# A 4096 x 4096 matrix product on one core: panels of half the width, chunked loads, and a transposed A kept in memory

## The chip, the core and the metric

The kernel runs on one core of one Trainium2 chip. Times are device microseconds from the first to the last work of a launch. TensorE (PE in the profile) multiplies and transposes, VectorE (DVE) copies, ScalarE (ACT) scales, GpSimd (POOL) issues the casting loads, and SyncE (SP) issues the other transfers. The accumulators that TensorE writes are PSUM tiles, everything else on the core is SBUF; `a`, `b` and `out` lie in the chip's memory.

## The reference

```python
def setup_inputs():
    m, k, n = 4096, 4096, 4096
    return {
        "a": np.random.randn(m, k).astype(np.float32),
        "b": np.random.randn(k, n).astype(np.float32),
        "scale": np.float32(0.1),
    }

def reference(a, b, scale):
    return np.matmul(a, b) * scale
```

## The kernel before, in words

B is cut into two panels of 2048 columns (`NB`, L27). For each panel one load from GpSimd's queue brings all 4096 rows into one SBUF tile and casts them to bf16 (L51). That tile has a single buffer, so the second panel's load waits until the first panel's last matmul is done. Inside a panel the loop runs over 32 blocks of 128 rows of A (L53). For each block:

- a load from GpSimd's queue brings 128 x 4096 of A, cast to bf16 (L56), into one of two buffers;
- TensorE transposes it in 32 pieces of 128 x 128 into PSUM tiles `pt` (L61), and VectorE copies each piece to the tile `at_sb` (L62); there are four `pt` buffers and two `at_sb` buffers;
- 4 x 32 matmuls of 128 x 512 (L67) add up into the one accumulator `po` of 128 x 2048, four column pieces one after the other;
- ScalarE multiplies `po` by the scale into `o_sb` (L76), and SyncE stores 1 MB of output (L77).

Each block of A is thus loaded and transposed twice, once for each panel. A scheduler orders each engine's instructions from this program and adds the waits; it puts the first transposes of a block ahead of and among the block's first matmuls. The single accumulator makes a block's first matmul wait for the scaling of the block before.

Of the kernel before, what the change touches and what calls it, by code (L numbers as in the profile page):

```python
# [1 line left out]

# [5 lines left out]


@with_exitstack
def kernel(
    ctx: ExitStack,
    tc: tile.TileContext,
    a: bass.AP,
    b: bass.AP,
    scale: float,
    out: bass.AP,
):
    nc = tc.nc  # L20
    P = 128
    M, K = a.shape
    K2, N = b.shape
    assert K == K2

    KO = K // P
    NB = 2048  # L27
    NPANELS = N // NB
    NSUB = NB // 512
    MB = M // P  # L30

    fp32 = mybir.dt.float32
    bf16 = mybir.dt.bfloat16

    b_r = b.rearrange("(ko ki) n -> ki ko n", ki=P)

    const = ctx.enter_context(tc.tile_pool(name="const", bufs=1))
    bpool = ctx.enter_context(tc.tile_pool(name="bpool", bufs=1))
    apool = ctx.enter_context(tc.tile_pool(name="apool", bufs=2))
    atpool = ctx.enter_context(tc.tile_pool(name="atpool", bufs=2))  # L40
    opool = ctx.enter_context(tc.tile_pool(name="opool", bufs=3))
    psum_o = ctx.enter_context(tc.tile_pool(name="psum_o", bufs=1, space=bass.MemoryType.PSUM))
    psum_t = ctx.enter_context(tc.tile_pool(name="psum_t", bufs=4, space=bass.MemoryType.PSUM))

    ident = const.tile([P, P], bf16)
    make_identity(nc, ident)

    for pi in range(NPANELS):
        n0 = pi * NB
        b_sb = bpool.tile([P, KO, NB], bf16, tag="bpanel")  # L50
        nc.gpsimd.dma_start(out=b_sb, in_=b_r[:, :, n0:n0 + NB])  # L51

        for mi in range(MB):  # L53
            m0 = mi * P
            a_sb = apool.tile([P, K], bf16, tag="arow")
            nc.gpsimd.dma_start(out=a_sb, in_=a[m0:m0 + P, :])  # L56

            at_sb = atpool.tile([P, KO, P], bf16, tag="at")
            for ko in range(KO):
                pt = psum_t.tile([P, P], bf16, tag="pt")  # L60
                nc.tensor.transpose(pt, a_sb[:, ko * P:(ko + 1) * P], ident)  # L61
                nc.vector.tensor_copy(at_sb[:, ko, :], pt)  # L62

            po = psum_o.tile([P, NB], fp32, tag="po", bufs=1)
            for ns in range(NSUB):
                for ko in range(KO):
                    nc.tensor.matmul(  # L67
                        po[:, ns * 512:(ns + 1) * 512],
                        at_sb[:, ko, :],
                        b_sb[:, ko, ns * 512:(ns + 1) * 512],  # L70
                        start=(ko == 0),
                        stop=(ko == KO - 1),
                    )

            o_sb = opool.tile([P, NB], fp32, tag="osb")
            nc.scalar.mul(o_sb, po, float(scale))  # L76
            nc.sync.dma_start(out=out[m0:m0 + P, n0:n0 + NB], in_=o_sb)  # L77


# [1 line left out]
_INS = ['a', 'b', 'scale']  # L81
_OUTS = [((4096, 4096), 'float32')]
#: Inputs that are plain numbers.
_NUMBERS = {'scale': 0.10000000149011612}


# [26 lines left out]
```

## Time and profile before

| | |
|---|---|
| median of 4 runs | 2159.67 us (2159.45 to 2160.71) |
| profiled execution | 2159.5 us |
| its span, first to last instruction | 2157.7 us |
| TensorE busy | 1934.5 us |
| VectorE busy | 324.9 us |
| ScalarE busy | 121.4 us |
| read from memory, written | 201.33 MB, 67.11 MB |
| mean granted TensorE clock | 0.981 |

Busy time of TensorE counts from a matmul's start to its modelled end, and matmuls overlap each other in the array; the time that a matmul costs is therefore the distance from one start to the next. The recorded mean of 379 ns for a 128 x 512 matmul is not that distance. Weight loads (PEld) are recorded completely and run beside the matmuls; some matmul records are missing, so counts are taken from the weight loads. The bytes of a casting load are counted as written, that is, as bf16.

### The profile page before, as it was taken

The numbers are of one execution on the slowest core, as the hardware profiler recorded it, in microseconds if no ns is written. First come the engines' busy times: TensorE is split into PE (matmuls) and PEld (weight loads), VectorE is DVE, ScalarE is ACT, GpSimd is POOL, SyncE is SP. The second block draws the span as 40 slices with busy tenths as digits, with TensorE's granted clock in tenths as the row PEclk, the third lists the DMA queues.
The fourth block names the chain that finished last, engine by engine and source line by source line (L and its number), as shares of the span: only waits on it lengthen the run. The fifth ranks groups of instructions, "written<-read, shape, count | busy, mean of one in ns | idle before, by whom it ended". The sixth has DMA issues, their size and how long they took to land.

```text
span 2157.7 us, 22825 instructions
## 1 busy us (share of the span) xinstructions
PE 1934.5 (90%) x10048; PEld 942.1 (44%) x10240; DVE 324.9 (15%) x2048; ACT 121.4 (6%) x65; POOL 38.2 (2%) x72
## 2 busy tenths in 40 slices
PE   0399999999999999999914999999999999999998
PEld 0144444444444444444411444444444444444444
DVE  0011111111111111111010011111111101110110
ACT  0000000000000000000000000000000000000000
POOL 0000000000000000000000000000000000000000
PEclk9999999999999999999966999999999999999999
DMA  9821332233223322332297222332233223322320
GB/s 198 172 70 48 79 78 68 50 78 79 65 53 79 79 63 55 79 79 61 57 208 162 59 65 53 79 79 63 55 78 79 61 57 78 79 61 57 79 59 40
DMA packets 26756, 169.26 MB, mean 78 GB/s; under 512 B 2080, under 2 KB 2080, under 8 KB 10272
## 3 DMA queue, kind: packets, MB, share of 16 engines
q0 software_dynamic: 17440, 100.67, 24.5%
q1 hardware_dynamic: 9216, 67.11, 7.6%
q8 instruction: 80, 1.31, 0.2%
q14 instruction: 20, 0.16, 0.0%
HBM read 201.33 MB, written 67.11 MB: 124 GB/s over the span
## 4 chain that ended last, share of the span: by engine, by line
PE 86%; another core or an unknown queue 8%; ACT 5%; issue 1%; DVE 0%; ACTq 0%
PE po L67 82%; ACT o_sb L76 5%; PE pt L61 4%; DVE at_sb L62 0%; ACTq L76 0%
## 5 line engine op out<-in xcount | busy, mean ns | idle before, releaser
L67 PE MATMUL po<-b_sb,at_sb 128*128 128x512 bf16 x8000 | 1826.3, 379 | 115.4 <-DMA b_sb<-in_b_dram 77.7
L67 PEld LDWEIGHTS <-at_sb 128*128 128x128 bf16 x8192 | 799.4, 98 | 969.3 <-DMA b_sb<-in_b_dram 77.9
L62 DVE COPY at_sb<-pt 128x128 bf16<-128x128 bf16 x2048 | 324.9, 219 | 1801.2 <-PE pt L61 1795.3
L61 PE MATMUL pt<-ident,a_sb 128*128 128x128 bf16 x2048 | 284.2, 219 | 101.0 <-DMA a_sb<-in_a_dram 88.6
L61 PEld LDWEIGHTS <-a_sb 128*128 128x128 bf16 x2048 | 191.4, 98 | 239.1 <-DMA a_sb<-in_a_dram 88.6
L76 ACT ACTIVATE o_sb<-po 128x2048 f32<-128x2048 f32 x64 | 120.1, 1877 | 2030.8 <-PE pt L61 1825.3
L56 POOL DMA_DIRECT2D a_sb<-in_a_dram x64 | 34.0, 532 | 2000.8 <-PE pt L61 1969.1
L51 POOL DMA_DIRECT2D b_sb<-in_b_dram x2 | 3.5, 1762 | 25.1 <-PE pt L61 24.7
L76 ACT ACT_TABLE_LOAD x1 | 1.3, 1283 | 0.7 <-PEq L94 0.7
masks.py:199 POOL TENSOR_SCALAR_AFFINE_SELECT ident<-ident 128x128 bf16<-128x128 bf16 x1 | 0.3, 307 | 0.1
masks.py:197 POOL MEMSET ident<- 128x128 bf16 x1 | 0.2, 205 | 0.3 <-POOLq L94 0.3
L94 POOL MEMSET const-float32-0.0<- 128x1 f32 x1 | 0.1, 100 | 0.2 <-issue 0.2
L94 POOL MEMSET const-bfloat16-1.0<- 128x1 bf16 x1 | 0.1, 103 | 0.0
L94 POOL MEMSET const-uint8-127<- 128x1 uint8 x1 | 0.1, 102 | 0.0
L94 POOL MEMSET const-float32-1.0<- 128x1 f32 x1 | 0.1, 100 | 0.0
## 6 DMA issues: line engine op xcount, KB each, us to landing
a_sb<-in_a_dram POOLq DMA_DIRECT2D x64, 1024.0 KB, 7.6
out_dram<-o_sb SPq DMA_DIRECT2D x64, 1024.0 KB, 3.9
b_sb<-in_b_dram POOLq DMA_DIRECT2D x2, 16384.0 KB, 84.1
```

The source lines that it names most:

```text
L51: nc.gpsimd.dma_start(out=b_sb, in_=b_r[:, :, n0:n0 + NB])
L56: nc.gpsimd.dma_start(out=a_sb, in_=a[m0:m0 + P, :])
L61: nc.tensor.transpose(pt, a_sb[:, ko * P:(ko + 1) * P], ident)
L62: nc.vector.tensor_copy(at_sb[:, ko, :], pt)
L67: nc.tensor.matmul(po[:, ns * 512:(ns + 1) * 512], at_sb[:, ko, :], b_sb[:, ko, ns * 512:(ns + 1) * 512], start=(ko == 0), stop=(ko == KO ...
L76: nc.scalar.mul(o_sb, po, float(scale))
L94: nc = _bacc.Bacc("TRN2", target_bir_lowering=False, num_devices=1)
```

## The change

- Panels are 1024 columns wide, so there are four. A panel of B is no longer one tile but 32 chunks of 128 x 1024, each with its own load, in a pool of 64 chunks, which holds two panels.
- In the first panel the first three blocks of A are loaded and transposed, then their 3 x 2 matmuls follow each chunk of B as it lands (`WIDE`). The load of the fourth block stands between chunks 21 and 22, its transposes behind chunk 26.
- Four transposes write one PSUM tile of 128 x 4 x 128, and one copy of 128 x 512 empties it; there are two such tiles.
- Each transposed block of A is written to a tile in memory (`at_dram`) by SyncE in the first panel; in the other panels it is read back from there, and neither loaded nor transposed again. There are four buffers for it.
- In the first panel the transposes of block t + 2 are placed behind the matmuls of chunk 4 of block t. The chunks of the second panel are spread over the blocks of the first.
- There are three accumulators of 128 x 1024. A block's two column pieces alternate for each chunk.

The order of the row-block work on TensorE. In the names, `a_6` is the seventh block of A, `pt_6_8` the PSUM tile of its pieces from 8 on, `po_0_4` the accumulator of panel 0, block 4; the number behind is the program's own. Before, in the second block:

```order
L67 MATMUL po_413<-b_sb_81,at_sb_316 128x512
L61 LDWEIGHTS a_sb_314
L61 MATMUL pt_386<-ident_76,a_sb_314 128x128 [waits DVE_49]
L61 LDWEIGHTS a_sb_314
L61 MATMUL pt_389<-ident_76,a_sb_314 128x128 [waits DVE_49]
L67 LDWEIGHTS at_sb_316
```

With the change, in block 4 of panel 0:

```order
L113 MATMUL po_0_4_732<-b_0_5_250,at_0_4_573 128x512
L69 LDWEIGHTS a_6_743
L69 MATMUL pt_6_8_758<-ident_79,a_6_743 128x128 [waits DVE_49]
...
L113 LDWEIGHTS at_0_4_573
L113 MATMUL po_0_4_732<-b_0_6_252,at_0_4_573 128x512
L69 LDWEIGHTS a_6_743
L69 MATMUL pt_6_12_764<-ident_79,a_6_743 128x128 [waits DVE_49]
```

One or two transposes of the same block stood between matmuls, each waiting for a copy; now four transposes of the block two further stand between single matmuls, and the first of each four waits for a copy.

The order of the loads on GpSimd's queue at the start of the program (`b_0_21` is chunk 21 of panel 0). Before:

```order
L51 DMA b_sb_81<-in_b_dram 128x32x2048
masks.py:199 ISA
masks.py:199 AFFINE_SELECT ident_76<-ident_76 128x128
L56 DMA a_sb_83<-in_a_dram 128x4096
L56 DMA a_sb_314<-in_a_dram 128x4096
```

With the change, behind the loads of A blocks 0 to 2 and chunks 0 to 20:

```order
L52 DMA b_0_21_282<-in_b_dram 128x1024
L58 DMA a_3_284<-in_a_dram 128x4096
L52 DMA b_0_22_286<-in_b_dram 128x1024
...
L52 DMA b_0_31_304<-in_b_dram 128x1024
L58 DMA a_4_571<-in_a_dram 128x4096
L58 DMA a_5_655<-in_a_dram 128x4096
L58 DMA a_6_743<-in_a_dram 128x4096
L52 DMA b_1_0_849<-in_b_dram 128x1024
```

A's first block stood behind the whole panel of B; now three blocks of A stand ahead of it, a fourth inside it and the next three behind it.

The order on SyncE's queue. Before it held the 64 output stores alone. With the change, in the second panel (`at_1_4` is the reload for its block 4, `o_1_0` its block 0's output):

```order
L76 DMA at_1_4_4200<-at_dram_78 128x4096 [waits DMAHW4_49,PE_49]
L109 DMA out_0_dram<-o_1_0_4125 128x1024 [waits Activation_49]
L76 DMA at_1_5_4272<-at_dram_78 128x4096 [waits DMAHW6_49,PE_49]
L109 DMA out_0_dram<-o_1_1_4197 128x1024 [waits DMAHW7_49,Activation_49]
L76 DMA at_1_6_4344<-at_dram_78 128x4096 [waits DMAHW0_49,PE_49]
```

Each reload now stands ahead of the store of the block whose buffer it takes over, and waits for TensorE to be done with that block.

```diff
--- before.py
+++ after.py
@@ -24,7 +24,7 @@
     assert K == K2
 
     KO = K // P
-    NB = 2048
+    NB = 1024
     NPANELS = N // NB
     NSUB = NB // 512
     MB = M // P
@@ -32,49 +32,131 @@
     fp32 = mybir.dt.float32
     bf16 = mybir.dt.bfloat16
 
-    b_r = b.rearrange("(ko ki) n -> ki ko n", ki=P)
+    const = ctx.enter_context(tc.tile_pool(name="const", bufs=1))
+    dram = ctx.enter_context(tc.tile_pool(name="dram", bufs=1, space=bass.MemoryType.DRAM))
+    bpool = ctx.enter_context(tc.tile_pool(name="bpool", bufs=2 * KO))
+    apool = ctx.enter_context(tc.tile_pool(name="apool", bufs=3))
+    atpool = ctx.enter_context(tc.tile_pool(name="atpool", bufs=4))
+    opool = ctx.enter_context(tc.tile_pool(name="opool", bufs=3))
+    psum_o = ctx.enter_context(tc.tile_pool(name="psum_o", bufs=3, space=bass.MemoryType.PSUM))
+    psum_t = ctx.enter_context(tc.tile_pool(name="psum_t", bufs=2, space=bass.MemoryType.PSUM))
 
-    const = ctx.enter_context(tc.tile_pool(name="const", bufs=1))
-    bpool = ctx.enter_context(tc.tile_pool(name="bpool", bufs=1))
-    apool = ctx.enter_context(tc.tile_pool(name="apool", bufs=2))
-    atpool = ctx.enter_context(tc.tile_pool(name="atpool", bufs=2))
-    opool = ctx.enter_context(tc.tile_pool(name="opool", bufs=3))
-    psum_o = ctx.enter_context(tc.tile_pool(name="psum_o", bufs=1, space=bass.MemoryType.PSUM))
-    psum_t = ctx.enter_context(tc.tile_pool(name="psum_t", bufs=4, space=bass.MemoryType.PSUM))
+    at_dram = dram.tile([MB, P, KO, P], bf16)
 
     ident = const.tile([P, P], bf16)
     make_identity(nc, ident)
 
-    for pi in range(NPANELS):
+    def load_b_chunk(pi, ko):
         n0 = pi * NB
-        b_sb = bpool.tile([P, KO, NB], bf16, tag="bpanel")
-        nc.gpsimd.dma_start(out=b_sb, in_=b_r[:, :, n0:n0 + NB])
+        bt = bpool.tile([P, NB], bf16, tag="bc", name=f"b_{pi}_{ko}")
+        nc.gpsimd.dma_start(out=bt, in_=b[ko * P:(ko + 1) * P, n0:n0 + NB])
+        return bt
 
-        for mi in range(MB):
-            m0 = mi * P
-            a_sb = apool.tile([P, K], bf16, tag="arow")
-            nc.gpsimd.dma_start(out=a_sb, in_=a[m0:m0 + P, :])
+    def load_a(mi):
+        m0 = mi * P
+        a_tiles[mi] = apool.tile([P, K], bf16, tag="arow", name=f"a_{mi}")
+        a_ins[mi] = nc.gpsimd.dma_start(out=a_tiles[mi], in_=a[m0:m0 + P, :]).ins
 
-            at_sb = atpool.tile([P, KO, P], bf16, tag="at")
-            for ko in range(KO):
-                pt = psum_t.tile([P, P], bf16, tag="pt")
-                nc.tensor.transpose(pt, a_sb[:, ko * P:(ko + 1) * P], ident)
-                nc.vector.tensor_copy(at_sb[:, ko, :], pt)
+    def make_at_via_pe(mi):
+        if mi not in a_tiles:
+            load_a(mi)
+        a_sb = a_tiles.pop(mi)
+        at_sb = atpool.tile([P, KO, P], bf16, tag="at", name=f"at_0_{mi}")
+        for kg in range(0, KO, 4):
+            pt = psum_t.tile([P, 4, P], bf16, tag="pt", name=f"pt_{mi}_{kg}")
+            for j in range(4):
+                ko = kg + j
+                nc.tensor.transpose(pt[:, j, :], a_sb[:, ko * P:(ko + 1) * P], ident)
+            nc.vector.tensor_copy(at_sb[:, kg:kg + 4, :], pt)
+        nc.sync.dma_start(out=at_dram[mi], in_=at_sb)
+        return at_sb
 
-            po = psum_o.tile([P, NB], fp32, tag="po", bufs=1)
-            for ns in range(NSUB):
-                for ko in range(KO):
-                    nc.tensor.matmul(
-                        po[:, ns * 512:(ns + 1) * 512],
-                        at_sb[:, ko, :],
-                        b_sb[:, ko, ns * 512:(ns + 1) * 512],
-                        start=(ko == 0),
-                        stop=(ko == KO - 1),
-                    )
+    def load_at(pi, mi):
+        at_sb = atpool.tile([P, KO, P], bf16, tag="at", name=f"at_{pi}_{mi}")
+        nc.sync.dma_start(out=at_sb, in_=at_dram[mi])
+        return at_sb
 
-            o_sb = opool.tile([P, NB], fp32, tag="osb")
-            nc.scalar.mul(o_sb, po, float(scale))
-            nc.sync.dma_start(out=out[m0:m0 + P, n0:n0 + NB], in_=o_sb)
+    def produce_at(pi, mi):
+        if pi == 0:
+            return make_at_via_pe(mi)
+        return load_at(pi, mi)
+
+    iters = [(pi, mi) for pi in range(NPANELS) for mi in range(MB)]
+    T = len(iters)
+    AHEAD = 2
+
+    a_ins = {}
+    a_tiles = {}
+    b_tiles = {}
+    at_tiles = {}
+
+    WIDE = 3
+    for s in range(WIDE):
+        at_tiles[s] = produce_at(*iters[s])
+    latest = WIDE - 1
+    for ko in range(KO):
+        if ko == 22:
+            latest += 1
+            load_a(latest)
+        with tc.issue_after(a_ins[latest]):
+            b_tiles[(0, ko)] = load_b_chunk(0, ko)
+
+    def finish(pi, mi, po):
+        n0 = pi * NB
+        m0 = mi * P
+        o_sb = opool.tile([P, NB], fp32, tag="osb", name=f"o_{pi}_{mi}")
+        nc.scalar.mul(o_sb, po, float(scale))
+        nc.sync.dma_start(out=out[m0:m0 + P, n0:n0 + NB], in_=o_sb)
+
+    def mm(po, at, pi, ko):
+        for ns in range(NSUB):
+            i = nc.tensor.matmul(
+                po[:, ns * 512:(ns + 1) * 512],
+                at[:, ko, :],
+                b_tiles[(pi, ko)][:, ns * 512:(ns + 1) * 512],
+                start=(ko == 0),
+                stop=(ko == KO - 1),
+            )
+        return i.ins
+
+    # the first WIDE row blocks follow the chunks of B as they land
+    pos = [psum_o.tile([P, NB], fp32, tag="po", name=f"po_0_{w}") for w in range(WIDE)]
+    for ko in range(KO):
+        for w in range(WIDE):
+            ins = mm(pos[w], at_tiles[w], 0, ko)
+        if ko == 26:
+            with tc.issue_after(ins):
+                at_tiles[WIDE] = produce_at(*iters[WIDE])
+    for w in range(WIDE):
+        finish(0, w, pos[w])
+        at_tiles.pop(w)
+
+    nb = 0
+    for t in range(WIDE, T):
+        pi, mi = iters[t]
+        ahead = [WIDE + 1, WIDE + 2] if t == WIDE else [t + 2] if t + 2 < T else []
+        if pi > 0:
+            for s in ahead:
+                at_tiles[s] = produce_at(*iters[s])
+            ahead = []
+            if pi + 1 < NPANELS:
+                b_tiles[(pi + 1, mi)] = load_b_chunk(pi + 1, mi)
+
+        at_cur = at_tiles.pop(t)
+        po = psum_o.tile([P, NB], fp32, tag="po", name=f"po_{pi}_{mi}")
+        for ko in range(KO):
+            ins = mm(po, at_cur, pi, ko)
+            if ko in (4, 20) and ahead:
+                with tc.issue_after(ins):
+                    s = ahead.pop(0)
+                    at_tiles[s] = produce_at(*iters[s])
+        if pi == 0:
+            want = KO if mi == MB - 1 else (mi - WIDE) * KO // (MB - WIDE)
+            with tc.issue_after(a_ins[max(a_ins)]):
+                while nb < want:
+                    b_tiles[(1, nb)] = load_b_chunk(1, nb)
+                    nb += 1
+        finish(pi, mi, po)
 
 
 # ---- launch: one core; inputs and outputs as the reference has them ----
```

## Rows read from the trace of the kernel before

**Rows 1.** The page, busy time of the engines and the transfer slices

```profile
PE 1934.5 (90%) x10048; PEld 942.1 (44%) x10240; DVE 324.9 (15%) x2048; ACT 121.4 (6%) x65; POOL 38.2 (2%) x72
...
DMA  9821332233223322332297222332233223322320
```

**Rows 2.** The waits of the whole span: us in total, times, longest

```profile
PE pt L61 <- DMA a_sb<-in_a_dram: 88.6, 1, 88.6
...
PE po L67 <- DMA b_sb<-in_b_dram: 77.7, 1, 77.7
...
PE po L67 <- ACT o_sb L76: 30.5, 61, 0.5
```

**Rows 3.** Groups by line: busy us, mean ns of one, idle before

```profile
L67 PE MATMUL po<-b_sb,at_sb 128*128 128x512 bf16 x8000 | 1826.3, 379 | 115.4 <-DMA b_sb<-in_b_dram 77.7 <-ACT o_sb L76 30.5 <-issue 0.2
L67 PEld LDWEIGHTS <-at_sb 128*128 128x128 bf16 x8192 | 799.4, 98 | 969.3 <-DMA b_sb<-in_b_dram 77.9 <-issue 3.5
L62 DVE COPY at_sb<-pt 128x128 bf16<-128x128 bf16 x2048 | 324.9, 219 | 1801.2 <-PE pt L61 1795.3
...
L76 ACT ACTIVATE o_sb<-po 128x2048 f32<-128x2048 f32 x64 | 120.1, 1877 | 2030.8 <-PE pt L61 1825.3 <-PE po L67 205.5
```

**Rows 4.** Timeline of one block of the second panel: start us, us

```profile
1285.12 1.68 PE L61 MATMUL pt<-ident,a_sb 128*128 128x128 bf16 x12
...
1287.84 0.28 PE L61 MATMUL pt<-ident,a_sb 128*128 128x128 bf16 x2
...
1287.95 0.38 PE L67 MATMUL po<-b_sb,at_sb 128*128 128x512 bf16 x1
...
1290.73 24.98 PEld L67 LDWEIGHTS <-at_sb 128*128 128x128 bf16 x117
1290.79 25.41 PE L67 MATMUL po<-b_sb,at_sb 128*128 128x512 bf16 x115
...
1316.04 1.67 PE L61 MATMUL pt<-ident,a_sb 128*128 128x128 bf16 x12
```

**Rows 5.** Timeline of the last block's end

```profile
2141.75 9.23 PE L67 MATMUL po<-b_sb,at_sb 128*128 128x512 bf16 x42
...
2152.97 0.33 SPq L77 DMA_DIRECT2D out_dram<-o_sb  x1
```

**Rows 6.** Stretches: us; PE, PEld, DVE, ACT, POOL busy (count); clock; DMA share; GB/s

```profile
0.00:88.60 88.60, 0.00 (x0) 0.00 (x0) 0.00 (x0) 1.28 (x1) 3.57 (x9) 1.00 1.02 205
1291.50:1298.50 7.00, 7.00 (x34) 3.17 (x33) 0.00 (x0) 0.00 (x0) 0.28 (x1) 1.00 0.83 152
1304.50:1311.50 7.00, 6.95 (x33) 3.10 (x32) 0.00 (x0) 0.00 (x0) 0.00 (x0) 1.00 0.00 0
1087.00:1165.00 78.00, 0.30 (x3) 0.13 (x2) 0.41 (x4) 0.00 (x0) 0.53 (x1) 0.52 1.06 221
1165.00:1180.00 15.00, 14.73 (x61) 6.46 (x62) 0.00 (x0) 0.00 (x0) 0.00 (x0) 0.89 0.57 119
```

**Rows 7.** The page's transfer queues: packets, MB, share of 16 engines

```profile
q1 hardware_dynamic: 9216, 67.11, 7.6%
```

**Rows 8.** Timeline of the start

```profile
1.29 1.83 POOL L51 DMA_DIRECT2D b_sb<-in_b_dram  x1 [0.35 <-issue]
...
89.28 0.63 PE L67 MATMUL po<-b_sb,at_sb 128*128 128x512 bf16 x1
...
93.31 0.38 PE L67 MATMUL po<-b_sb,at_sb 128*128 128x512 bf16 x1
```

**Rows 9.** Landings of the A loads (L56), then of B's (L51)

```profile
DMA to landing us min/median/max: 7.4/7.6/89.4
...
DMA to landing us min/median/max: 82.5/84.1/85.8
```

**Rows 10.** Timeline of a stage with transposes alone

```profile
1078.57 8.58 PE L61 MATMUL pt<-ident,a_sb 128*128 128x128 bf16 x64
1078.83 8.59 DVE L62 COPY at_sb<-pt 128x128 bf16<-128x128 bf16 x64 [25.01 <-PE pt L61]
```

## The prediction

> **What bounds the kernel now.** I read the page first: TensorE is busy for 90% of a span of 2157.7 us, and the transfer engines are near their limit in only two places, at the start and in the middle [rows 1]. The waits say what these places are: TensorE waits once for 88.6 us, until the first row block of A lands behind the first panel of B, and once for 77.7 us, until the second panel of B lands; a third wait, for ScalarE, is short but comes 61 times and adds up to 30.5 us [rows 2]. The groups by line then give the counts [rows 3]: 8192 matmul pairs (the matmul row shows 8000, since some records are missing, but its weight loads show 8192), 2048 transposes, 2048 copies of them.
>
> The prices come from the timeline of one block [rows 4]. From 1290.79 to the next block's first transpose at 1316.04 stand 117 matmuls (counted by their weight loads): 25.25 / 117 = 0.2158 us each. The block begins at 1285.12 and the next at 1316.04, so a block is 30.92 us, of which 128 x 0.2158 = 27.62 are matmuls and 3.30 are transposes and the wait for ScalarE. A transpose between matmuls takes TensorE (1287.95 - 1287.84) / 2 = 0.055 us; I use 0.057. So the span is 88.6 + 77.7 of waiting, 8192 x 0.2158 = 1767.9 of matmuls, 6.7 of tail (last matmul ending at 2141.75 + 9.23 = 2150.98, span end 2157.7 [rows 5]), and 216.8 that is left, 3.39 for each of 64 blocks. The bound is thus TensorE's matmul time, which the change leaves as it is; what can be won is the other 390 us.
>
> **The change part by part.** The 8192 matmuls stay, each with its weight load. Their pace also holds while transfers run: in 7 us with a DMA share of 0.83 there are 33 weight loads, in 7 us with none 32, both at clock 1.00, the upper level of 2.4 GHz [rows 6]. I cost the denser transfers at nothing here.
>
> *The second panel's wait goes.* Panels are now 1024 wide, and the next panel's chunks go into free buffers while this one is multiplied. In panel 0 a block has 13.81 us of matmuls (64 x 0.2158) and about 2.6 us of transposes. Its transfers are one A block of 1.05 MB at 205 GB/s (5.1 us [rows 6]), 1.1 chunks (1.4 us), one write of the transposed block and half as large an output. A MB-sized hardware-queue transfer costs 7.6% x 2157.7 / 64 = 2.56 us of all 16 engines [rows 7], so 2.56 + 1.28. That is 10.4 of 16.4 us: hidden. In panels 1 to 3 a block needs 2.56 + 1.28 + 1.3 = 5.1 of 13.81. SP's order shows a reload waiting only for the block four before its own to end, some 41 us ahead of its use; the output store behind it waits for ScalarE after that same block anyway. What is late next: nothing by these rows; without that cover the price is whatever a reload takes over 13.81 us per block.
>
> *The start.* The first A block is issued where B's load now is, at 1.29 [rows 8], and lands 7.6 us later [rows 9]: 8.9. After that three A blocks and 32 chunks of B, 11.53 MB as written, must land; at 205 GB/s that is 56.2 us, to 65.1. Into the same engines go the writes of the first three transposed blocks (7.7) and half of the fourth (1.3): 74.1. Chunks have packets half as large as any of B's now, which no row shows; I add 1 us: the last chunk lands at 75. TensorE's own work behind the first chunk (about 23 us in) is 192 x 0.2158 = 41.4, plus 2.5 for A block 3's transposes, plus about 2 for slow matmuls after idleness (0.63 us recorded at 89.28 against 0.38 at 93.31 [rows 8]; the granted clock, 0.52 in the second wait (near the lower level of 1.2 GHz), is still only 0.89 in the 15 us behind it [rows 6]): 69. So the transfers decide. After the last chunk come its six matmuls (1.3) and about 1 us of backlog from the transposes that stand at chunk 26: 77.3. Row block 3 then waits about 0.5 us for ScalarE to free the first of three accumulators, and runs ten matmuls (2.2), to 80.0. Its next work, in TensorE's order, is the transposes of A block 4, which is queued behind the last chunk: 75 + 5.1 + about 1.5 for the stores beside it = 81.6. That stall of 1.6 us is the new wait.
>
> *The transposes.* 1024 instead of 2048, as each A block is transposed once; 28 row blocks of transposes stand after the start. They come in groups of four for one 128x512 copy, over two accumulator banks, with seven matmuls between them. What a 128x512 copy takes no row shows. A single 128x128 copy takes 219 ns [rows 3]; in the stage where nothing else runs, 64 follow each other in 8.59 us, 0.134 each, with TensorE waiting for them [rows 10]. If the step between copies grows with the columns, it is 0.534, and a copy takes 0.62. I then walk through one row block: group 0 at 0, group 1 at 0.23, copy 0 starts 0.42 and ends 1.04, group 2 can start at 1.10 (0.06 for the signal), and each later group 0.55 after the one before, so the eighth ends at 4.07. Seven matmuls (1.51) ran meanwhile: 2.55 us of cost. The lower end is TensorE alone, 32 x 0.057 = 1.83; the upper end is four whole single copies per group, 0.876, with no overlap, and comes to 4.2. I take 2.55, as the 64-copy row is the nearest. 28 x 2.55 = 71.4.
>
> The Trainium skill has a rule here: "VectorE: DVE Perf Modes", section "Why PSUM operands drop a tier", caps an operand in PSUM at a twofold mode and does not rule that mode out for 16-bit data; by it the sum would be the first rival's. The 0.134 of [rows 10] is just 128 columns at one per cycle of the 0.96 GHz that this page of the Trainium skill gives, which speaks for no such mode, though a fixed part could hide it.
>
> *The wait for ScalarE* (30.5 us) goes: three accumulators instead of one. Without that cover it would be about 0.5 per block.
>
> *The tail.* The scaling of 128x1024 takes between half and all of the 1.877 us of 128x2048 [rows 3]; I take 1.0. The last store took 2157.7 - 2152.97 = 4.73 us to the end [rows 5]; half the bytes save 1.28. With 0.1 of signals: 4.6.
>
> **The sum.** 81.6 to the first transposes of block 3; 8192 - 202 = 7990 matmuls, 1724.2; 71.4; 4.6: 1881.8 us of span. The profiled execution's time is 1.8 above its span (2159.5 against 2157.7) and 0.2 us under the median of 2159.67, so I forecast 1884 us.
>
> **The rivals.**
> *Copies run twice as fast.* The 64-copy row [rows 10] also fits a step half of which is fixed, 0.067, and half of which grows with the columns. Then a large copy's step is 0.067 + 4 x 0.067 = 0.334, and TensorE's own order paces a row block and the cost is its lower end, 1.84: 28 x 0.71 = 20 less, 1864. Chance 12%.
>
> *The chunks do not overlap.* One load of a whole panel becomes 32 loads. If each paid its fixed part alone, 7.6 - 5.1 = 2.5 us [rows 6, 9], the start would be 32 x 2.5 = 80 longer: 1964. Against it: POOL's order lets a chunk wait only for the load eight before it, and the two A loads behind the first panel were issued long before it landed (its landing took 85.8, theirs up to 89.4 [rows 9]). Chance 8%. The Trainium skill speaks for it: "DMA: Bandwidth & Descriptors", section "Bandwidth", wants transfers of a MiB or more, and its section "Anatomy of one DMA — SWDGE (gpsimd) path" puts about 2 us of fixed time on each; by that page of the Trainium skill alone an estimate of the price would be 32 x 2 = 64 us, to 1948. The trace agrees on the fixed part, with its 2.5, and shows no chunk of this size.
>
> *The way through memory is slow.* In panels 1 to 3 every block needs a 1 MB reload of transposed A. If a reload moved as the 4096 runs of 256 bytes that its tile has in rows of 128, each taking a hardware packet's 7.6% x 2157.7 x 16 / 9216 = 0.285 us, it would last 4096 x 0.285 / 16 = 73 us, and 96 blocks would be 59 us longer each: over 7500 us. It decides as soon as a reload takes more than 13.81 us, and makes the kernel slower than before from 13.81 + (2159.5 - 1884) / 96 = 16.7 us. Against it: the writer and the reader use the same layout, 8 KB in a row for each partition, and the output's rows of that length cost 2.56 per MB. Chance 2%.
>
> **How the numbers follow.** The forecast with its bounds has 78%, the fast copies 12%, the lone chunks 8%, the slow memory 2%. The start can be about 10 us shorter (TensorE's own 69 plus 2.2, if the writes cost the stream nothing) or some 10 longer (slower small packets, a clock that falls in the pauses between chunks); the transposes 20 less or, at their upper end, 46 more; small waits of 0.1 us per block would add 12. I take 1858 to 1915: it holds the fast copies and leaves out the lone chunks, the far end of the copies and the slow memory. A measurement of this kernel tells about 0.2% (4 us) from no change. All but the last rival lie far below: faster 0.97, same 0.01, slower 0.02.
>
> **What would show it.** The profile after should have one long wait of TensorE (for the first A block, about 9 us), then short ones for chunks until about 77; 64 weight loads per 13.8 us with no gap in panels 1 to 3; 256 copies at about 0.62 us; transposed row blocks about 16.4 us apart in panel 0; ScalarE's scaling near 1.0 us with no one waiting. Copies at 0.42 mean the first rival; chunks landing 3 us apart the second; waits for reloads after 550 us the third. A matmul pace other than 0.2158 would break the whole sum, as 1% of it is 18 us.

## The result, and the profile after

The changed kernel takes 1864.66 us (median of 8 runs, 1863.97 to 1865.33) against 2159.84 for the kernel before beside it: a ratio of 0.8633, 95% interval 0.8625 to 0.8642. The forecast was 1884 with a range from 1858 to 1915. The profiled execution took 1864.53, with a span of 1862.8.

The page, busy time and transfer slices (before: [rows 1]):

```profile
PE 1826.2 (98%) x9034; PEld 862.8 (46%) x9216; DVE 106.0 (6%) x256; ACT 132.1 (7%) x129; POOL 85.6 (5%) x166
...
DMA  9997777778396334333359343343333433333331
```

TensorE is busy for 98% of the span, and the middle stretch of full transfer slices is gone. The waits (us in total, times, longest; before: [rows 2]):

```profile
PE pt L69 <- DMA a<-in_a_dram: 11.9, 2, 9.5
...
PE po L113 <- DMA b<-in_b_dram: 8.9, 4, 4.6
...
PE po L113 <- ACT o L108: 0.2, 1, 0.2
```

The 88.6 and 77.7 us have become 11.9 and 8.9, and the 30.5 for ScalarE is 0.2. The groups by line (busy, mean ns of one | idle before; before: [rows 3]):

```profile
L113 PEld LDWEIGHTS <-at 128*128 128x128 bf16 x8192 | 799.6, 98 | 942.5 <-issue 9.3
L108 ACT ACTIVATE o<-po 128x1024 f32<-128x1024 f32 x128 | 130.9, 1024 | 1726.3 <-PE po L113 1675.2 <-remote 51.2
L70 DVE COPY at<-pt 128x512 bf16<-128x512 bf16 x256 | 106.0, 424 | 388.7 <-PE pt L69 381.3
```

There are 256 copies of 512 columns, and one takes 424 ns, not the 620 of the forecast. The start, in order of time (start us, us; before: [rows 8]):

```profile
9.46 4.33 PE L69 MATMUL pt<-ident,a 128*128 128x128 bf16 x32 [9.46 <-DMA a<-in_a_dram]
...
24.86 0.58 PE L113 MATMUL po<-b,at 128*128 128x512 bf16 x1 [3.15 <-DMA b<-in_b_dram]
...
62.63 8.32 PE L113 MATMUL po<-b,at 128*128 128x512 bf16 x30 [4.57 <-DMA b<-in_b_dram]
...
78.44 2.85 ACT L108 ACTIVATE o<-po 128x1024 f32<-128x1024 f32 x3 [76.42 <-PE po L113]
...
79.52 2.32 PE L113 MATMUL po<-b,at 128*128 128x512 bf16 x9 [0.25 <-ACT o L108]
...
81.67 0.61 PE L69 MATMUL pt<-ident,a 128*128 128x128 bf16 x8
```

The first transposes begin at 9.46, the first matmul at 24.86 and, after a pause of 4.57 us, TensorE goes on at 62.63. Scaling of the first block starts at 78.44, block 3's matmuls at 79.52, and the transposes inside block 3 at 81.67, where the forecast had 81.6. Stretches behind that pause, in the second panel while chunks are loaded, and in the last panels (columns as in [rows 6]):

```profile
62.70:66.50 3.80, 3.80 (x11) 1.33 (x11) 0.00 (x0) 0.00 (x0) 1.59 (x3) 0.55 1.12 209
66.50:70.80 4.30, 4.30 (x22) 1.94 (x21) 0.00 (x0) 0.00 (x0) 0.53 (x1) 1.00 1.12 209
520.00:620.00 100.00, 99.47 (x455) 45.36 (x464) 0.00 (x0) 7.17 (x7) 15.93 (x31) 1.00 0.79 205
1100.00:1800.00 700.00, 696.58 (x3180) 317.36 (x3244) 0.00 (x0) 51.20 (x50) 0.00 (x0) 1.00 0.36 115
```

In the last 700 us are 3244 weight loads, 0.2158 us each; in 100 us with a DMA share of 0.79 there are 464, 0.2155 each. The pace is that of [rows 4]. Behind the pause the granted clock is 0.55 for 3.8 us, near the lower level of 1.2 GHz, and then 1.00, the upper level of 2.4 GHz. Two row blocks of the first panel, by the start of their transposes ([rows 4] before), and then the end ([rows 5] before):

```profile
99.19 0.61 PE L69 MATMUL pt<-ident,a 128*128 128x128 bf16 x8
...
114.85 0.61 PE L69 MATMUL pt<-ident,a 128*128 128x128 bf16 x8
```

```profile
1834.64 23.47 PE L113 MATMUL po<-b,at 128*128 128x512 bf16 x106
...
1858.20 1.02 ACT L108 ACTIVATE o<-po 128x1024 f32<-128x1024 f32 x1 [12.79 <-PE po L113]
```

A row block in panel 0 takes 114.85 - 99.19 = 15.66 us, so its transposes cost 15.66 - 13.81 = 1.85. The last matmul ends at 1858.11, and 4.7 us of tail follow.

**Where the 295 us went.** Both spans hold 8192 x 0.2158 = 1767.9 us of matmuls. Beside them the kernel before had 389.8: 166.3 in two waits, 216.8 in transposes, waits for ScalarE and slow matmuls, 6.7 of tail. The changed one has 94.9: up to 81.67 it did 202 matmuls (43.6), so 38.1 went to waits, the slow clock and four blocks' transposes; then 28 x 1.85 = 51.8, and 4.7 of tail. The waits for B's second panel and for A's first block are read from the wait rows alone; no run below puts B's whole panels or the single copies back.

### The profile page after: what moved, and what is told of

Read it like the earlier page. It is cut to its first block, busy times and chain, and to the rows that moved or that the text cites. A ratio compares the mean times of both kernels' runs of the same rounds, so it can differ in the third digit from the quotient of the medians.

```text
span 1862.8 us, 19601 instructions
## 1 busy us (share of the span) xinstructions
PE 1826.2 (98%) x9034; PEld 862.8 (46%) x9216; DVE 106.0 (6%) x256; ACT 132.1 (7%) x129; POOL 85.6 (5%) x166
## 4 chain that ended last, share of the span: by engine, by line
PE 95%; DMA 3%; issue 1%; DVE 0%; ACT 0%; POOL 0%; POOLq 0%; ACTq 0%
PE po L113 93%; PE pt L69 3%; DMA b<-in_b_dram 2%; DMA a<-in_a_dram 1%; DVE at L70 0%; ACT o L108 0%; POOL a L58 0%; POOL ident masks.py:199 0%; POOL ident masks.py:197 0%; POOLq masks.py:199 0%; ACTq L108 0%; POOLq L176 0%
## 5 line engine op out<-in xcount | busy, mean ns | idle before, releaser
L113 PE MATMUL po<-b,at 128*128 128x512 bf16 x8010 | 1789.4, 379 | 17.8 <-DMA b<-in_b_dram 8.9
L113 PEld LDWEIGHTS <-at 128*128 128x128 bf16 x8192 | 799.6, 98 | 942.5 <-issue 9.3
L108 ACT ACTIVATE o<-po 128x1024 f32<-128x1024 f32 x128 | 130.9, 1024 | 1726.3 <-PE po L113 1675.2
L70 DVE COPY at<-pt 128x512 bf16<-128x512 bf16 x256 | 106.0, 424 | 388.7 <-PE pt L69 381.3
L69 PE MATMUL pt<-ident,a 128*128 128x128 bf16 x1024 | 96.6, 225 | 14.2 <-DMA a<-in_a_dram 11.9
L69 PEld LDWEIGHTS <-a 128*128 128x128 bf16 x1024 | 78.2, 100 | 52.3 <-DMA a<-in_a_dram 12.9
L52 POOL DMA_DIRECT2D b<-in_b_dram x128 | 68.1, 538 | 567.7 <-PE po L113 478.1
L58 POOL DMA_DIRECT2D a<-in_a_dram x32 | 17.1, 535 | 355.4 <-PE pt L69 352.4
## 6 DMA issues: line engine op xcount, KB each, us to landing
b<-in_b_dram POOLq DMA_DIRECT2D x128, 256.0 KB, 13.3
```

The costliest lines, as they stand in the source:

```text
L52: nc.gpsimd.dma_start(out=bt, in_=b[ko * P:(ko + 1) * P, n0:n0 + NB])
L58: a_ins[mi] = nc.gpsimd.dma_start(out=a_tiles[mi], in_=a[m0:m0 + P, :]).ins
L69: nc.tensor.transpose(pt[:, j, :], a_sb[:, ko * P:(ko + 1) * P], ident)
L70: nc.vector.tensor_copy(at_sb[:, kg:kg + 4, :], pt)
L113: i = nc.tensor.matmul(po[:, ns * 512:(ns + 1) * 512], at[:, ko, :], b_tiles[(pi, ko)][:, ns * 512:(ns + 1) * 512], start=(ko == 0), stop= ...
```

## The experiments

**How a copy's time grows.** Behind each group's own copy, some blocks copy the same tile again, in pieces of one size, to a scratch tile that nothing reads.

```diff
             nc.vector.tensor_copy(at_sb[:, kg:kg + 4, :], pt)
+            if mi % 4 == 1:
+                for j in range(4):
+                    nc.vector.tensor_copy(scr[:, 0, j * P:(j + 1) * P], pt[:, j, :])
...
```

> Behind each group's own copy, blocks of A whose number is 1, 2 or 3 modulo 4 copy the same accumulator tile once more to a scratch tile that nothing reads, in 4 copies of 128 columns, 2 of 256 or 2 of 512, with no wait for TensorE between them. Theory F (a fixed 0.067 us and 1.92 columns per ns of step): 0.22, 0.29 and 0.425 us long, steps of 0.134, 0.20 and 0.334 us. Theory G (the forecast's: one column per cycle, all of the step grows): steps of 0.134, 0.267 and 0.534 us. Theory H (the step of 0.134 before was the round trip of four buffers, not the copy): the 128-column copies step clearly below 0.134, 0.07 to 0.1 us.

The extra copies by line: 512, 128 and 256 columns wide (busy, mean ns of one | idle before):

```profile
L81 DVE COPY scr<-pt 128x512 bf16<-128x512 bf16 x128 | 47.8, 415 | 0.0
L75 DVE COPY scr<-pt 128x128 bf16<-128x128 bf16 x256 | 39.0, 215 | 0.0
L78 DVE COPY scr<-pt 128x256 bf16<-128x256 bf16 x128 | 30.7, 282 | 0.0
```

Idle time before them is 0.0, so nothing but VectorE sets their step. The timeline of VectorE shows it (start, us, count):

```profile
74.32 0.74 DVE L81 COPY scr<-pt 128x512 bf16<-128x512 bf16 x2
74.98 0.41 DVE L72 COPY at<-pt 128x512 bf16<-128x512 bf16 x1
...
91.75 0.61 DVE L75 COPY scr<-pt 128x128 bf16<-128x128 bf16 x4
92.27 0.41 DVE L72 COPY at<-pt 128x512 bf16<-128x512 bf16 x1
```

Two copies of 512 from 74.32 to the next at 74.98: 0.33 each. Four of 128 from 91.75 to 92.27: 0.13 each. In the trace's records the steps are 0.131, 0.198 and 0.331 us for 128, 256 and 512 columns. The rows above give the same: each size has 64 groups (8 blocks with 8 groups each), and for 256 columns 30.7 / 64 = 0.480 us for two copies, less one of 0.282, is a step of 0.198. They lie on one line: 0.064 us fixed and 0.200 us for 384 more columns, 1.92 columns per ns. Theory F holds at all three sizes. G, the growth on which the forecast rested, fails at 0.331 against 0.534; H fails too, since the 128-column step is the same with no buffer to wait for. The whole run (one launch) took 1864.16 us, so the extra copies cost nothing that can be told: VectorE is idle enough. The Trainium skill, "VectorE: DVE Perf Modes", section "Why PSUM operands drop a tier", allows a twofold mode for an operand in PSUM; 1.92 columns per ns is twofold at the 0.96 GHz of that page, so the trace agrees with it.

**Without the way through memory.**

```diff
-        nc.sync.dma_start(out=at_dram[mi], in_=at_sb)
...
-        if pi == 0:
-            return make_at_via_pe(mi)
-        return load_at(pi, mi)
+        return make_at_via_pe(pi * MB + mi)
```

> Every panel loads and transposes A anew; nothing is written to or read back from memory but the inputs and the output. Theory A (a transposed block costs TensorE 1.85 us wherever it stands): 96 x 1.85 = 178 us more, about 2042 us. Rival (transposes in the later panels fall into time that TensorE has to spare): below 1900 us. Second rival (A's loads take the place as the bound in panels 1 to 3): above 2060 us.

It took 2031.52 us (one launch), 166.9 more than the changed kernel. ScalarE's scalings (start, us) show why it is not 178:

```profile
67.84 2.86 ACT L105 ACTIVATE o<-po 128x1024 f32<-128x1024 f32 x3 [65.81 <-PE po L110]
...
713.18 1.02 ACT L105 ACTIVATE o<-po 128x1024 f32<-128x1024 f32 x1 [14.64 <-PE po L110]
728.84 1.02 ACT L105 ACTIVATE o<-po 128x1024 f32<-128x1024 f32 x1 [14.64 <-PE po L110]
```

Two blocks in the second panel lie 728.84 - 713.18 = 15.66 us apart, where the changed kernel has 13.81: 1.85 for each of 96 blocks, 177.6, as theory A says. But the first scaling comes at 67.84 instead of 78.44. This kernel writes no transposed block into the stream of chunks, and that alone makes its start 10.6 us shorter: 177.6 - 10.6 = 167.0. Both rivals fall.

**One accumulator.**

```diff
-        po = psum_o.tile([P, NB], fp32, tag="po", name=f"po_{pi}_{mi}")
+        po = pos[0]
```

> All blocks behind the start use one accumulator instead of taking turns among three. Theory A (without the cover each of 125 blocks waits for the whole scaling, 1.02 us and about 0.3 of signals): about 165 us more, about 2030 us. Rival, the price that the forecast put on the missing cover (0.5 us per block, as before the change): about 1927 us.

It took 2028.47 us (one launch). TensorE's wait (total, times, longest) and two scalings:

```profile
PE po L113 <- ACT o L108: 144.7, 125, 1.5
```

```profile
705.25 1.02 ACT L108 ACTIVATE o<-po 128x1024 f32<-128x1024 f32 x1 [14.11 <-PE po L113]
720.38 1.02 ACT L108 ACTIVATE o<-po 128x1024 f32<-128x1024 f32 x1 [14.11 <-PE po L113]
```

A block takes 15.13 us instead of 13.81, 1.32 more, and 125 x 1.32 = 165; the run is 163.8 longer than the changed kernel. Theory A holds. The forecast's price for the missing cover, 0.5 us per block, was too low: before the change the scheduler filled most of that wait with the next block's transposes ([rows 4] begins with them), and in this kernel there is nothing to fill it with.

**Three blocks or one beside the stream.**

```diff
-    WIDE = 3
+    WIDE = 1
```

> One block of A instead of three follows the chunks of B as they land. Theory A (what counts is the TensorE work that lies beside the stream): chunk 31 lands near 60 us, with only 64 matmuls behind it; 202 matmuls and four transposed blocks are reached at about 97 us instead of 81.7, so about 1880 us. Rival (TensorE's work is the same in all and the stream ends sooner, so the wide start brings nothing): 1865 us or less.

It took 1879.29 us (1877.87 to 1879.77). The first 58 us (columns as in [rows 6]):

```profile
0.00:58.00 58.00, 31.39 (x124) 12.69 (x127) 6.28 (x16) 1.28 (x1) 19.82 (x42) 0.71 1.04 203
```

TensorE is granted 0.71 of its clock there, between its two levels, while it gets two matmuls for each chunk and waits for the next. Theory A's 1880 holds: the wide start is worth 14.6 us.

**Block 3's load ahead of the chunks.**

```diff
-        if ko == 22:
+        if ko == 0:
```

> The load of A block 3 stands ahead of all chunks of B instead of between chunks 21 and 22. The bytes ahead of the last chunk are the same. Theory A (the transfers alone decide when the start ends): no change, 1864 to 1865 us. Theory B (TensorE's pause of 4.6 us for that load drops its clock, and from there TensorE is the later one until the start ends): no pause, no fall of the clock, 2 to 3 us less, about 1862 us.

It took 1865.33 us (1863.18 to 1865.72), ratio 0.8633 with 0.8621 to 0.8645: no change, as theory A says. But not for its reason. TensorE's timeline and a stretch:

```profile
32.05 0.58 PE L113 MATMUL po<-b,at 128*128 128x512 bf16 x1 [8.22 <-DMA b<-in_b_dram]
...
78.73 1.45 PE L113 MATMUL po<-b,at 128*128 128x512 bf16 x6 [0.25 <-ACT o L108]
```

```profile
20.00:37.50 17.50, 8.21 (x41) 4.44 (x40) 3.30 (x8) 0.00 (x0) 2.58 (x5) 0.61 1.05 290
```

The wait has moved in front: TensorE stands for 8.22 us until chunk 0 at 32.05, and from 20 to 37.5 its clock is 0.61. From 35.15 it then runs without a wait to the end of the start, so here it is TensorE and not the stream that decides; block 3 begins at 78.73 instead of 79.52, which is 0.8 us and not theory B's 2 to 3. Theory B was right that the pause makes TensorE late, and wrong that it can be had for nothing: the same 5 us of transfer stand in front of the first chunk instead.

**Late writes.**

```diff
     for w in range(WIDE):
-        finish(0, w, pos[w])
+        stored = finish(0, w, pos[w])
+    for w in range(WIDE):
+        with tc.issue_after(stored):
+            nc.sync.dma_start(out=at_dram[w], in_=at_tiles[w])
         at_tiles.pop(w)
```

The three blocks are no longer written where they are made, and there are five buffers for transposed A instead of four.

> The writes of the first three transposed A blocks are queued behind the first output stores instead of into the stream of B's chunks. Theory A (each write costs the chunk stream about 2 us, as the gaps of 3.6 and 3.3 us between chunks instead of 1.26 say): the start is 5 to 6 us shorter, about 1859 us. Rival (the two queues together move more than one alone, so a write costs the stream nothing): no change, 1864 to 1865 us.

It took 1871.46 us (1870.61 to 1871.77), 6.8 more; both theories missed. The timeline says why (TensorE's rows, and ScalarE's first scalings):

```profile
53.88 6.63 PE L114 MATMUL po<-b,at 128*128 128x512 bf16 x30 [3.74 <-DMA b<-in_b_dram]
...
68.01 2.85 ACT L109 ACTIVATE o<-po 128x1024 f32<-128x1024 f32 x3 [65.99 <-PE po L114]
...
96.17 0.58 PE L69 MATMUL pt<-ident,a 128*128 128x128 bf16 x4 [15.01 <-DVE at L70]
```

The first scalings come at 68.01 instead of 78.44: the start won 10.4 us, more than theory A's 5 to 6. Then TensorE stands for 15.01 us, until 96.17, for a copy. The late writes' own rows name what that copy waited for, and their landings:

```profile
  DVE at L70: 20.3, 1
...
DMA to landing us min/median/max: 24.3/26.8/28.8
```

VectorE waits 20.3 us for a write: the block-5 copies take over block 0's buffer, and the three writes, queued at 71.3 to 72.3 among the stores and the loads of A that follow, land 24 to 29 us later. 1864.66 - 10.4 + 15.0 = 1869.3 leaves about 2 us, which fits the slow matmuls behind the wait: the granted clock is 0.50, the lower level, from 96.1 to 100.0.

**A in quarters between the chunks, late writes too.** The first four blocks of A are loaded 1024 columns at a time, one piece behind every other chunk, and each quarter is transposed just ahead of its chunks:

```diff
+    pieces = {1: (0, 1), 3: (1, 1), 5: (2, 1), 9: (0, 2), 11: (1, 2), 13: (2, 2),
+              17: (0, 3), 19: (1, 3), 21: (2, 3),
+              23: (3, 0), 25: (3, 1), 27: (3, 2), 29: (3, 3)}
...
+            if ko in pieces:
+                load_quarter(*pieces[ko])
```

> The first four blocks of A are loaded in quarters of K between the chunks of B, each quarter transposed just ahead of its chunks, and the first three writes come late as in the run on late writes. If the start is decided by bytes and by TensorE's pauses, the first matmul comes at about 10 us instead of 25, chunk 31 lands at about 64, the four blocks are transposed and three multiplied by about 67.5 instead of 79.5: about 1853 us. Rival (small A pieces or the many transposes between chunks cost as much as they save): 1860 us or more.

It took 1873.56 us (1872.45 to 1874.59), beyond the rival's 1860 and 2.1 longer than late writes alone. TensorE's rows and the first scalings:

```profile
10.78 7.02 PE L144 MATMUL po<-b,at 128*128 128x512 bf16 x24 [0.21 <-DMA b<-in_b_dram]
...
98.35 1.01 PE L69 MATMUL pt<-ident,a 128*128 128x128 bf16 x8 [15.73 <-DVE at L70]
```

```profile
67.41 2.85 ACT L139 ACTIVATE o<-po 128x1024 f32<-128x1024 f32 x3 [65.39 <-PE po L144]
```

The first matmul does come at 10.78, against 20.32 with late writes alone, but the first scaling, at 67.41, only 0.6 us earlier than there: TensorE still follows the stream to its end. Block 3's transposes now stand behind the stream, from 68.08 to 71.44, instead of inside it, and the same wait for a buffer follows, 15.73 us (there are four buffers here). So the forecast of 1853 fails mainly by that wait, and the rival is not refuted: what the quarters save at the front is lost again by the end, and how much of that is the price of the small pieces this run doesn't tell.

**Late writes with six buffers.**

```diff
-    bpool = ctx.enter_context(tc.tile_pool(name="bpool", bufs=2 * KO))
+    bpool = ctx.enter_context(tc.tile_pool(name="bpool", bufs=2 * KO - 4))
...
-    atpool = ctx.enter_context(tc.tile_pool(name="atpool", bufs=4))
+    atpool = ctx.enter_context(tc.tile_pool(name="atpool", bufs=6))
...
     for w in range(WIDE):
-        finish(0, w, pos[w])
+        stored = finish(0, w, pos[w])
+        with tc.issue_after(stored):
+            nc.sync.dma_start(out=at_dram[w], in_=at_tiles[w])
```

> As the run on late writes, but with six buffers for transposed A instead of five (the room comes from the pool of B's chunks, 60 instead of 64), and each late write queued right behind the output store of its own block. Theory A (the late writes won 10.4 us at the start and lost it again since block 5's copies waited 15 us for a buffer whose write had not landed): the first scaling comes at about 68 us, no such wait, about 1854 us. Rival (any delay of the writes meets the later loads, and the wait only moves to another place): 1864 us or more.

> The changed kernel again, beside the run before it on the same chip, so that half a per cent between the two can be told: 1864 to 1866 us by every theory.

It took 1854.00 us (1853.70 to 1854.85), and the changed kernel on the same chip 1864.89 (1863.78 to 1865.14). Against the kernel before, the ratio is 0.8584, 0.8572 to 0.8596. Its first scalings, the wait that was to go, and the late writes' landings:

```profile
68.04 2.85 ACT L109 ACTIVATE o<-po 128x1024 f32<-128x1024 f32 x3 [66.02 <-PE po L114]
```

```profile
PE pt L69 <- DVE at L70: 0.5, 1, 0.5
```

```profile
DMA to landing us min/median/max: 17.2/26.5/35.4
```

The first scalings stand at 68.04, and TensorE waits 0.5 us in all for copies. Theory A's 1854 holds: the buffer wait was what the late writes had paid with, and this version beats both kernels. Two things that bear on this wait were changed at once, and no run separates them. Block 0's write, issued at 69.51, landed 17.2 us later, at 86.7, against 95.6 in the run on late writes; and its buffer is wanted by block 6, whose copies start at 89.33, no longer by block 5, whose transposes stand at 80.1. By these rows, five buffers with the new order would still have waited some 6 us (an estimate), and so would six with the old one.

## Why the prediction was right, step by step

The time lies in the range because the range took in the first rival, to which the forecast gave 12%. The forecast's own choice for the copies failed, and the start came out to 0.1 us partly by luck.

**The matmuls' pace** held at 0.2158, also beside the transfers of [rows 6], and with it the sum.

**The second wait and the reloads.** Blocks in panels 1 to 3 lie 13.81 us apart, and TensorE waits for no reload. The issues and their landings (KB each, median us to landing; [rows 9] before):

```profile
at<-at_dram SPq DMA_DIRECT2D x96, 1024.0 KB, 5.9
...
b<-in_b_dram POOLq DMA_DIRECT2D x128, 256.0 KB, 13.3
```

A reload lands 5.9 us after it is issued, against the 13.81 from which it would decide: the slow way through memory was no danger. A single chunk takes 13.3 to land, but that is time in the queue. Around the pause GpSimd's issues (start, us, what it waited for) show the chunks' own step:

```profile
61.62 0.53 POOL L52 DMA_DIRECT2D b<-in_b_dram  x1 [4.57 <-DMA a<-in_a_dram]
...
62.87 0.53 POOL L52 DMA_DIRECT2D b<-in_b_dram  x1 [0.72 <-DMA b<-in_b_dram]
...
64.11 0.53 POOL L52 DMA_DIRECT2D b<-in_b_dram  x1 [0.72 <-DMA b<-in_b_dram]
```

From 62.87 to 64.11 is 1.24 us for 0.262 MB, 211 GB/s, the rate of the whole panel before [rows 6]; the packets of half the size cost nothing. So the rival in which chunks do not overlap is out. The Trainium skill's rule of a MiB or more, "DMA: Bandwidth & Descriptors", section "Bandwidth", does not bind here: with up to eight such loads queued, chunks of 256 KB as written move at 211 GB/s, where the load of a whole panel moved at 205.

**The start** came out at 81.67 against 81.6, but two of its parts missed and cancelled, a pause that came and a stall that did not. The first block landed in time for transposes at 9.46 (8.9). The last chunk, issued at 64.11, landed 9.7 us later, at 73.9 (75); with late writes it was issued at 55.42 and landed at 65.2. So the three writes cost the stream 8.7 us (7.7). TensorE lost 10.4 to them: the other 1.7 us is its clock, since the 30 matmuls recorded behind the pause took 8.32 us here and 6.63 with late writes, where the pause was 3.74 us.

Missed was the pause itself. Block 3's load lies in the queue between chunks 21 and 22. The chunk issued at 48.96, right behind that load, is the one that TensorE waits for at 62.63:

```profile
  PE po L113: 4.6, 1
...
DMA to landing us min/median/max: 13.6/13.6/13.6
```

The load's 1.05 MB, 5.1 us at the 205 GB/s of [rows 6], stood between two chunks, so TensorE stood for 4.57 us, ran at a clock of 0.55 behind it, and from there had no further wait for a chunk: it ended the three blocks 5 us behind the last chunk. So TensorE decided at the end, and not the transfers as the forecast had it. That moved the end of the three blocks from 77.3 to 79.3, and hid the landing of A block 4, the forecast's new wait of 1.6 us, which did not come.

**The transposes are the term that was mis-sized.** The step "If the step between copies grows with the columns, it is 0.534, and a copy takes 0.62" failed: a copy takes 0.425, and the step has a fixed part of 0.064. So TensorE's own order paces a row block, at 1.85 and not 2.55 us, and 28 x 0.70 = 19.6 us is the difference between forecast and result (19.3). This is the first rival, with its step of 0.334 against a measured 0.331, and its time of 1864. The single row [rows 10] on which the choice was made gave a step at one size; it could not tell a fixed part from growth, and the forecast took the end that it called nearest. (The forecast's upper end, walked with 0.876 from the first copy on, is 4.45 and not 4.2; nothing hangs on it.)

**The wait for ScalarE** is 0.2 us in all. The price put on its cover was too low, 0.5 instead of 1.32. **The tail** is 4.7 (4.6), with 1.024 us for the scaling.

## What to carry to other kernels

A step measured at one size doesn't say how it grows: before scaling it up, ask for the fixed part, or forecast both ends. A bulk write that nobody waits for still costs when it is put into a stream that somebody waits for; to move it later takes buffers enough to wait for its landing under load, not its time alone. An engine that starts earlier on a stream wins nothing while the stream still ends at the same time: with the quarters the first matmul came 9.5 us earlier than with late writes, and the first scaling 0.6.

## What the runs showed of the hardware that was not expected

- A copy from an accumulator tile in bf16 steps by 0.064 us plus 0.521 ns for each column, at 128, 256 and 512 columns.
- A write of 1 MB of transposed A lands 3.9 us after its issue at best (changed kernel). With casting loads and output stores queued beside it, it took 24.3 to 28.8 us in the run on late writes and up to 38.3 in the run with six buffers.
- Behind a pause of TensorE of 4.57 us the granted clock was 0.55 over the next 3.8 us (near the lower level of 1.2 GHz), then 1.00. Behind the pause of 3.74 us in the run on late writes 30 matmuls took 6.63 us, the pace of the upper level of 2.4 GHz. In the kernel before, the stage with 64 transposes in 8.6 us [rows 10] ran at clock 1.00 (1078.5 to 1087.2 of that trace).
